# Two heads' keys summed while the tokens still land, with products of the identity ahead of them

## The chip, the cores and the metric

The kernel runs on one core of a Trainium2 chip. The metric is the device time of one execution in microseconds (us). The engines of a core work side by side, each through its own queue in order: TensorE (PE, matrix products, with its weight loads shown as PEld), VectorE (DVE), ScalarE (ACT), GpSimd (POOL), and SyncE (SP), which here only issues transfers (DMAs).

## What is computed

The kernel is one decoder block on 16 meta tokens and 512 tokens (528 in all) of width 1024. The part that matters here is its beginning: a root-mean-square norm, one large projection, and of that projection the gated-delta branch with 8 heads.

```python
n = _rmsnorm(h, pre_mix_norm[l])
proj = jnp.einsum('btd,dn->btn', n, w_in[l])
(gq, gk, gv, gz, gb, ga, aq, ak, av, iq, ik, iw, gate_a, gate_b) = jnp.split(proj, split_at, axis=-1)
...
qkv = jax.nn.silu(_causal_conv(jnp.concatenate([q, k, v], axis=-1), conv_w))
...
k = _l2norm(k)
beta = jax.nn.sigmoid(b_raw)
g = -jnp.exp(a_log) * jax.nn.softplus(a_raw + dt_bias)
...
gc = jnp.cumsum(g, axis=-1)
decay = jnp.exp(jnp.where(tri_incl, gc[..., :, None] - gc[..., None, :], -jnp.inf))
A = jnp.where(tri_strict, jnp.einsum('bhncd,bhnsd->bhncs', kb, k) * decay, 0.0)
```

Sparse attention, the merge and the MLP follow; the change doesn't touch them.

## The kernel before

Tokens lie transposed: `xr` holds 8 slices of 128 channels by 528 tokens, landing as 8 transfers of 264 KB. For each slice `k`, ACT writes its scaled high part `nhi`, DVE the remainder `nlo`, and POOL or ACT the square `sq`, which DVE sums into `sqs`. The norm's factor per token is not applied to the input; it is computed later from `sqs` and multiplied into the results as the row vector `rb`.

Weights come by `wload`: SP loads up to 512 KB into one of two buffers `raw`, ACT casts the high part (`hi_...`, line 99), DVE subtracts for the low part (`lo_...`, line 100). A projection (`proj_a`, lines 194 to 196) makes three products per slice, high by high, high by low and low by high, for each half of the tokens (264 columns): 48 products for one tile of up to 128 output columns. PE's results go to PSUM, in a ring of three buffers for projections (`pp`) and one of five for the rest (`sp`).

In order of the program: the "small columns" (`misc`, 88 columns: the index key, the raw beta and decay inputs, the index weights); from `sqs` the norm's factors (`ssn`, line 152, and the square-root chain on DVE), spread into `rb` by the products `pc` and `pb` (lines 164 to 168); from the small columns beta and the decay `gg` with a chain of small DVE operations (lines 223 to 240); its cumulated sums by the products `gcp` (lines 245 to 248). From these, POOL's queue writes `gcd` to memory and reads it back broadcast as the eight tiles `E` (line 273) and, behind them, `zsp` (line 276), from which DVE makes the decay's exponents (`decay_abs`, lines 282 and 119; `zsp`, line 277).

Meanwhile `keys(h)` projects the keys of head `h` (`pa_k`), copies them out (line 297), multiplies by `rb` (line 299), runs the convolution of four taps (ACT line 300, three DVE operations, line 303), silu and square on ACT (lines 305 and 328), and the norm's products `kss` (line 335). All silus wait until the last exponential of the decay's chain (`last_exp`) is done. The values (`pa_v`) come next.

The order of instructions on each engine is made when the kernel is built: a scheduler orders by priorities and its own estimates, and `issue_after` keeps one behind another. On the chip the order of each queue is fixed.

Of the kernel before, what the change touches and what calls it, by code (L numbers as in the profile page):

```python
# [31 lines left out]
TOPK = 128  # L32
IDX_H = 8
IDX_D = 64
S4 = {"a": 4 * T, "b": 4 * L}


@with_exitstack
def hybrid_block(ctx: ExitStack, tc: tile.TileContext, io: dict):
# [6 lines left out]
    def f(ap):  # L46
        return ap.bitcast(F32)
# [12 lines left out]
    def ptile(name, p=None):  # L60
        return (p or pp).tile([P, 512], F32, tag="ps", name=name)
# [122 lines left out]
    def proj_a(w, name, moving=None, m=P, full=True, first=0):  # L184

        hi, lo = w
        mh, ml, base = moving if moving is not None else (nhi, nlo, 0 if full else NM)
        marks.clear()
        n2 = (T - first) // 2
        parts = [(ptile(f"pa_{name}_{i}"), first + i * n2, n2) for i in range(2)] if full else [(ptile(f"pa_{name}"), 0, L)]  # L190
        for pt, c, n in parts:
            for k in range(KT):
                ws, ms = slice(k * m, (k + 1) * m), slice(base + c, base + c + n)
                TE.matmul(pt[:m, :n], hi[:, ws], mh[:, k, ms], start=(k == 0), stop=False)  # L194
                TE.matmul(pt[:m, :n], hi[:, ws], ml[:, k, ms], start=False, stop=False)  # L195
                mark = TE.matmul(pt[:m, :n], lo[:, ws], mh[:, k, ms], start=False, stop=(k == KT - 1))  # L196
                if k == KT - 1:
                    marks.append(mark)
        return parts


    misc = const("misc", [96, T])
    G.memset(misc[64:96, :], 0.0)
    for pt, c, n in proj_a(w_misc, "misc", m=88):
        S.copy(misc[:88, c : c + n], pt[:88, :n])
    scp = stile("scp")
    for t in range(1, 5):
        c, n = tokcols(t)
# [79 lines left out]
    def conv(g, c0, parts_of, out, name, wide=False):

        if wide:  # L290
            both = wk.tile([P, 2, T], F32, tag="tb", name=f"cb_{name}", bufs=2)
            cv, y = both[:, 0, :], both[:, 1, : T - c0]
        else:
            cv = wk.tile([P, T], F32, tag="cv", name=f"cv_{name}", bufs=2)
            y = wk.tile([P, T], F32, tag="y", name=f"cy_{name}", bufs=2)[:, : T - c0]
# [937 lines left out]
```

## Time and profile before

| | |
|---|---|
| three runs | 1062.56, 1062.84, 1065.58 us; median 1062.84 |
| the profiled execution | 1063.86 us, its span 1062.2 us from first to last instruction |
| PE busy | 1040.1 us, 98% of the span, 6249 products |
| DVE busy | 682.0 us, 64% |
| ACT busy | 460.9 us, 43% |
| POOL busy | 61.7 us, 6% |
| DMA | 96.44 MB |

Busy time says how long an engine had something running. Of an engine with 98% only the few stretches where it idles or runs slowly can shrink, so one looks for where these are: PE's busy share is under nine tenths only in the first and the last of 40 slices of the span.

### The profile page before, as it was taken

What the parts mean: (1) busy time and instruction counts of PE and PEld (TensorE: products, weight loads), DVE (VectorE), ACT (ScalarE), POOL (GpSimd) and SP (SyncE); (2) the same over time, 40 slices, a digit from 0 to 9 for tenths busy, and PEclk for the clock granted to TensorE, in tenths of its full rate; (3) what the DMA queues carried; (4) which work ended last, traced back from release to release, by engine and by line L of the source; (5) the groups of instructions that cost most, each with busy time, mean ns of one, the idle gap of its engine ahead of it and who ended that gap; (6) DMA issues with size and microseconds to landing.
All of it is one profiled execution on the core that took longest, in us unless ns stands there. A gap on an engine that the chain in (4) does not pass through costs nothing.

```text
span 1062.2 us, 15893 instructions
## 1 busy us (share of the span) xinstructions
PE 1040.1 (98%) x6249; PEld 900.7 (85%) x6249; DVE 682.0 (64%) x1502; ACT 460.9 (43%) x854; POOL 61.7 (6%) x85
## 2 busy tenths in 40 slices
PE   6999999999999999999999999999999999999996
PEld 6999999999997888898888888898888888888885
DVE  6797899516789999857967464794431343343346
ACT  5555565443268722346755332473432431242131
POOL 4202302100000000000000000000000000000022
PEclk9999999998999999999999999999999999999999
DMA  5433424210123133322111325133233323332332
GB/s 180 134 102 95 124 86 134 63 41 2 41 83 117 46 94 99 100 80 80 60 60 41 99 93 204 60 103 95 84 96 99 96 85 98 99 90 88 99 99 80
DMA packets 28235, 96.44 MB, mean 91 GB/s; under 512 B 3632, under 2 KB 3968, under 8 KB 28160
## 3 DMA queue, kind: packets, MB, share of 16 engines
q1 hardware_dynamic: 25440, 87.51, 26.5%
q0 software_dynamic: 2720, 7.92, 2.9%
q8 instruction: 49, 0.80, 0.3%
q14 instruction: 26, 0.21, 0.1%
HBM read 90.14 MB, written 5.28 MB: 90 GB/s over the span
## 4 chain that ended last, share of the span: by engine, by line
PE 89%; DVE 5%; ACT 2%; DMA 2%; issue 1%; SPq 0%; DVEq 0%; ACTq 0%
PE up L1103 5%; PE up L1104 5%; PE up L1102 5%; PE d L505 4%; PE d L504 4%; PE d L506 4%; PE pa_dense L891 2%; PE pa_dense L890 2%; PE pa_dense L889 2%; PE pa_q L196 1%; PE pa_q L194 1%; PE pa_q L195 1%; PE pa_bg L194 1%; PE pa_bg L196 1%; PE pa_bg L195 1%; PE bd L1012 1%
## 5 line engine op out<-in xcount | busy, mean ns | idle before, releaser
L1103 PE MATMUL up<-n2l,hi_up 128*128 128x512 f32 (+1 forms) x288 | 106.9, 372 | 0.0
L1102 PE MATMUL up<-n2h,hi_up 128*128 128x512 f32 (+1 forms) x288 | 106.6, 371 | 0.0
L1104 PE MATMUL up<-n2h,lo_up 128*128 128x512 f32 (+1 forms) x288 | 106.6, 371 | 0.0
L100 DVE TENSOR_TENSOR lo_up<-raw_up,hi_up 128x1024 fp32r<-128x1024 f32 x32 | 39.2, 1226 | 71.1 <-PE up L1103 52.9
L100 DVE TENSOR_TENSOR lo_d<-raw_d,hi_d 128x1024 fp32r<-128x1024 f32 x24 | 29.4, 1227 | 78.4 <-PE d L505 56.0
L504 PE MATMUL d<-hi_d,uh 128*128 128x512 f32 x192 | 75.9, 396 | 0.0
L506 PE MATMUL d<-hi_d,ul 128*128 128x512 f32 x192 | 75.9, 395 | 0.0
L505 PE MATMUL d<-lo_d,uh 128*128 128x512 f32 x192 | 75.9, 395 | 0.0
L1106 ACT ACTIVATE rup<-up 128x512 f32<-128x512 f32 (+1 forms) x36 | 19.9, 552 | 99.5 <-PE up L1104 99.4
L1103 PEld LDWEIGHTS up<-n2l,hi_up 128*128 128x128 f32 x288 | 54.2, 188 | 10.3
L1102 PEld LDWEIGHTS up<-n2h,hi_up 128*128 128x128 f32 x288 | 54.2, 188 | 10.3
L1104 PEld LDWEIGHTS up<-n2h,lo_up 128*128 128x128 f32 x288 | 54.1, 188 | 10.3
L99 ACT CAST hi_d<-raw_d 128x1024 fp32r<-128x1024 f32 x24 | 25.2, 1050 | 59.6 <-PE d L506 59.6
L99 ACT CAST hi_up<-raw_up 128x1024 fp32r<-128x1024 f32 x32 | 33.4, 1045 | 24.6 <-PE d L506 22.7
L504 PEld LDWEIGHTS d<-hi_d,uh 128*128 128x128 f32 x192 | 36.1, 188 | 8.8
L506 PEld LDWEIGHTS d<-hi_d,ul 128*128 128x128 f32 x192 | 36.1, 188 | 8.7
L505 PEld LDWEIGHTS d<-lo_d,uh 128*128 128x128 f32 x192 | 36.1, 188 | 8.7
L889 PE MATMUL pa_dense<-nhi,hi_dense 128*128 128x512 f32 x96 | 39.3, 409 | 0.0
L890 PE MATMUL pa_dense<-nlo,hi_dense 128*128 128x512 f32 x96 | 38.0, 396 | 0.0
L548 PE MATMUL pb_z<-hi_z,nhi 128*128 128x256 f32 x128 | 38.0, 297 | 0.0
L891 PE MATMUL pa_dense<-nhi,lo_dense 128*128 128x512 f32 x96 | 38.0, 396 | 0.0
L194 PE MATMUL pa_k<-nhi,hi_k 128*128 128x264 f32 x128 | 37.1, 290 | 0.0
(570 smaller groups left out, 3075.6 us busy)
## 6 DMA issues: line engine op xcount, KB each, us to landing
raw_up<-w_up SPq DMA_DIRECT2D x32, 512.0 KB, 3.6
raw_d<-w_down SPq DMA_DIRECT2D x24, 512.0 KB, 3.6
raw_k<-w_k SPq DMA_DIRECT2D x8, 512.0 KB, 4.6
raw_v<-w_v SPq DMA_DIRECT2D x8, 512.0 KB, 4.4
raw_q<-w_q SPq DMA_DIRECT2D x8, 512.0 KB, 3.6
raw_z<-w_z SPq DMA_DIRECT2D x8, 512.0 KB, 3.6
raw_w_ga<-w_ga SPq DMA_DIRECT2D x8, 512.0 KB, 3.6
raw_bg<-w_bg SPq DMA_DIRECT2D x8, 512.0 KB, 3.6
```

The costliest lines, as they stand in the source:

```text
L99: S.copy(hi[:, :n], raw[:, :n])
L100: V.tensor_tensor(lo[:, :n], raw[:, :n], f(hi[:, :n]), ALU.subtract)
L194: TE.matmul(pt[:m, :n], hi[:, ws], mh[:, k, ms], start=(k == 0), stop=False)
L504: TE.matmul(pt, lh, whi, start=beg, stop=False)
L505: TE.matmul(pt, lh, wlo, start=False, stop=False)
L506: TE.matmul(pt, ll, whi, start=False, stop=end)
L889: TE.matmul(pt, hi[:, ws], nhi[:, k, NM:], start=(k == 0), stop=False)
L890: TE.matmul(pt, hi[:, ws], nlo[:, k, NM:], start=False, stop=False)
L891: mm = TE.matmul(pt, lo[:, ws], nhi[:, k, NM:], start=False, stop=(k == KT - 1))
L1102: TE.matmul(pt, hi[:, ws], n2h[:, k, ms], start=(k == 0), stop=False)
L1103: TE.matmul(pt, hi[:, ws], n2l[:, k, ms], start=False, stop=False)
L1104: TE.matmul(pt, lo[:, ws], n2h[:, k, ms], start=False, stop=(k == KT - 1))
```

## The change

The keys of heads 0 and 1 (`NHEAD = 2`) are no longer projected by `keys(h)`. Their weights come with those of the small columns in four pieces (`head_weights`: 176 columns of `w_misc` and 512 of `w_k`, 352 KB in two transfers), one ahead of every second slice of tokens. As a slice lands, PE adds its part to the sums of the small columns and of both heads (`head_part`, `heads`: 6 products each), in six PSUM buffers `hd00` to `hd21`, for slices 0 to 3. For slices 4 to 7 it adds only the small columns' part; the heads' parts of those four follow behind slice 7. `issue_after(last_head.ins)` holds these products to that order, and 26 products of the identity by itself stand ahead of them. The small columns' sums and the heads' sums are then copied out, the latter to the buffers of the convolution (`conv_columns`).

```diff
+    heads = [(0, 88)] + [(2 * 88 + 2 * P * i, P) for i in range(NHEAD)]
+    hps = [[ptile(f"hd{i}{x}", sp if 2 * i + x < 3 else pp) for x in range(2)] for i in range(NHEAD + 1)]
+    for _ in range(26):
+        last_head = TE.matmul(hps[NHEAD][1][:, :P], ident, ident, start=True, stop=True)
+    def head_weights(k):
+        n = 2 * 88 + 2 * P * NHEAD
+        raw = wp.tile([P, 1024], F32, tag="raw", name=f"raw_head{k}", bufs=2)
+        nc.sync.dma_start(raw[:, : 2 * 88], io["w_misc"][:, k * 88 : (k + 2) * 88])
+        nc.sync.dma_start(raw[:, 2 * 88 : n].rearrange("p (h c) -> p h c", h=NHEAD), io["w_k"][:NHEAD, :, k * P : (k + 2) * P].rearrange("h p c -> p h c"))
+        hi, lo = HW[k // 2]
+        S.copy(hi[:, :n], raw[:, :n])
+        V.tensor_tensor(lo[:, :n], raw[:, :n], f(hi[:, :n]), ALU.subtract)
...
+    def head_part(i, k):
+        nonlocal last_head
+        o, m = heads[i]
+        hi, lo = HW[k // 2]
+        ws = slice(o + k % 2 * m, o + k % 2 * m + m)
+        for x in range(2):
+            ms = slice(x * HT, x * HT + HT)
+            for a, b in ((hi, nhi), (hi, nlo), (lo, nhi)):
+                with tc.issue_after(last_head.ins):
+                    mm = TE.matmul(hps[i][x][:m, :HT], a[:, ws], b[:, k, ms], start=(k == 0 and a is hi and b is nhi), stop=(k == KT - 1 and a is lo))
+        last_head = mm
     for k in range(KT):
         nc.sync.dma_start(xr[:, k, :], io["hT"][:, k, :])
-        if k == 0:
-            w_misc = wload(io["w_misc"], 8 * 88, "misc")
+        if k % 2 == 0:
+            head_weights(k)
...
+        for i in range(NHEAD + 1) if k < KT // 2 else (0,):
+            head_part(i, k)
...
-    for pt, c, n in proj_a(w_misc, "misc", m=88):
-        S.copy(misc[:88, c : c + n], pt[:88, :n])
+    for x in range(2):
+        S.copy(misc[:88, x * HT : x * HT + HT], hps[0][x][:88, :HT])
+    for i in range(1, NHEAD + 1):
+        for k in range(KT // 2, KT):
+            head_part(i, k)
+    headc = []
+    for i in range(NHEAD):
+        headc.append(conv_columns(f"k{i}"))
+        for x in range(2):
+            S.copy(headc[i][0][:, x * HT : x * HT + HT], hps[1 + i][x][:, :HT])
...
     def keys(h):
-        w = wload(io["w_k"][h], 1024, f"k{h}")
-        parts = proj_a(w, f"k{h}")
-        later(1, 0)
-        sq = conv(8 + h, 0, parts, kT[:, h, :], f"k{h}", wide=h % 4 > 1)
+        if h < NHEAD:
+            sq = conv(8 + h, 0, [], kT[:, h, :], f"k{h}", columns=headc[h])
+        else:
+            parts = proj_a(wload(io["w_k"][h], 1024, f"k{h}"), f"k{h}")
+            later(1, 0)
+            sq = conv(8 + h, 0, parts, kT[:, h, :], f"k{h}", wide=h % 4 > 1)
```

Three places show how the scheduler's order moves. First PE where the norm's sums `ssn` are made. Before, they stand among the products of head 0's second half:

```order
L194 MATMUL pa_k0_1_348<-nhi_98,hi_k0_343 128x264
L195 MATMUL pa_k0_1_348<-nlo_99,hi_k0_343 128x264
L152 MATMUL ssn_212<-one_84,sqs_101 16x1
L152 MATMUL ssn_212<-one_84,sqs_101 128x1 x4
L196 MATMUL pa_k0_1_348<-nhi_98,lo_k0_344 128x264
```

After, behind all products of the head (the last is that of `hd21`) and the transposes of the small columns, `scp`; the next products are those of head 2:

```order
L161 MATMUL hd21_110<-nhi_98,lo_head3_144 128x264
L260 MATMUL scp_360<-ident_78,misc_300 128x32 x4
L261 MATMUL scp_360<-ident_78,misc_300 16x32
L188 MATMUL ssn_368<-one_84,sqs_101 16x1
L188 MATMUL ssn_368<-one_84,sqs_101 128x1 x4
L230 MATMUL pa_k2_0_517<-nhi_98,hi_k2_513 128x264
```

So `ssn` and all that hangs on it stand behind two whole heads, where before they stood inside the first. `gcp` moves too, from among head 2's products to behind the third product of head 4.

Second, DVE around the low part of head 6's weights, `lo_k6`. Before, from the low part of head 5's weights to that of head 6's:

```order
L100 TENSOR_TENSOR lo_k5_705<-raw_k5_702,hi_k5_704 128x1024
L303 SCALAR_TENSOR_TENSOR cb_k3_613<-cb_k3_613,convw_92 128x527
L277 TENSOR_TENSOR zsp_326<-zsp_326,gc_292 16x128
L303 SCALAR_TENSOR_TENSOR cb_k3_613<-cb_k3_613,convw_92 128x526
L119 TENSOR_SCALAR zsp_326<-zsp_326 16x128
L303 SCALAR_TENSOR_TENSOR cb_k3_613<-cb_k3_613,convw_92 128x525
L282 TENSOR_TENSOR E_317<-E_317,gc_292 128x512
L299 TENSOR_TENSOR cv_k4_687<-cv_k4_687,rb_100 128x528
L119 TENSOR_SCALAR E_317<-E_317 128x512
L282 TENSOR_TENSOR E_317<-E_317,gc_292 128x512
L100 TENSOR_TENSOR lo_k6_784<-raw_k6_781,hi_k6_783 128x1024
```

After, the same stretch is longer: its first part runs from `lo_k5` and the first tile of `E` to the last tap of head 4, and the second from there over `zsp` to `lo_k6`:

```order
L101 TENSOR_TENSOR lo_k5_741<-raw_k5_738,hi_k5_740 128x1024
L333 TENSOR_TENSOR E_473<-E_473,gc_448 128x512
L350 SCALAR_TENSOR_TENSOR cb_k3_649<-cb_k3_649,convw_92 128x527
L346 TENSOR_TENSOR cv_k4_723<-cv_k4_723,rb_100 128x528
L350 SCALAR_TENSOR_TENSOR cb_k3_649<-cb_k3_649,convw_92 128x526
L120 TENSOR_SCALAR E_473<-E_473 128x512
L350 SCALAR_TENSOR_TENSOR cb_k3_649<-cb_k3_649,convw_92 128x525
L350 SCALAR_TENSOR_TENSOR y_k4_724<-cv_k4_723,convw_92,y_k4_724 128x527
L333 TENSOR_TENSOR E_473<-E_473,gc_448 128x512
L350 SCALAR_TENSOR_TENSOR y_k4_724<-cv_k4_723,convw_92,y_k4_724 128x526
L120 TENSOR_SCALAR E_473<-E_473 128x512
L350 SCALAR_TENSOR_TENSOR y_k4_724<-cv_k4_723,convw_92,y_k4_724 128x525
```

```order
L328 TENSOR_TENSOR zsp_482<-zsp_482,gc_448 16x128
L346 TENSOR_TENSOR cv_k5_802<-cv_k5_802,rb_100 128x528
L120 TENSOR_SCALAR zsp_482<-zsp_482 16x128
L333 TENSOR_TENSOR E_473<-E_473,gc_448 128x512 x2
L350 SCALAR_TENSOR_TENSOR y_k5_803<-cv_k5_802,convw_92,y_k5_803 128x527
L120 TENSOR_SCALAR E_473<-E_473 128x512
L350 SCALAR_TENSOR_TENSOR y_k5_803<-cv_k5_802,convw_92,y_k5_803 128x526
L120 TENSOR_SCALAR E_473<-E_473 128x512
L350 SCALAR_TENSOR_TENSOR y_k5_803<-cv_k5_802,convw_92,y_k5_803 128x525
L101 TENSOR_TENSOR lo_k6_820<-raw_k6_817,hi_k6_819 128x1024
```

Before, `lo_k6` stands ahead of head 4's taps, with three tiles of `E` begun; now it stands behind four tiles of `E`, `zsp` and all taps of heads 4 and 5.

Third, PE where head 6 begins. Before:

```order
L196 MATMUL pa_k5_1_709<-nhi_98,lo_k5_705 128x264
L335 MATMUL kss3_758<-one_84,cb_k3_613 16x1
L335 MATMUL kss3_758<-one_84,cb_k3_613 128x1 x4
L194 MATMUL pa_k6_0_787<-nhi_98,hi_k6_783 128x264
L195 MATMUL pa_k6_0_787<-nlo_99,hi_k6_783 128x264
L196 MATMUL pa_k6_0_787<-nhi_98,lo_k6_784 128x264
```

After:

```order
L232 MATMUL pa_k5_1_745<-nhi_98,lo_k5_741 128x264
L230 MATMUL pa_k6_0_823<-nhi_98,hi_k6_819 128x264
L231 MATMUL pa_k6_0_823<-nlo_99,hi_k6_819 128x264
L230 MATMUL pa_k6_1_824<-nhi_98,hi_k6_819 128x264
L384 MATMUL kss3_794<-one_84,cb_k3_649 16x1
L384 MATMUL kss3_794<-one_84,cb_k3_649 128x1 x4
L231 MATMUL pa_k6_1_824<-nlo_99,hi_k6_819 128x264
L230 MATMUL pa_k7_0_901<-nhi_98,hi_k7_897 128x264
L232 MATMUL pa_k6_0_823<-nhi_98,lo_k6_820 128x264
```

The products that need no low part, one of head 7 among them, have moved ahead of the first that reads `lo_k6`. From the values of head 0 on, the orders of PE before and after are the same but for one row.

## Rows read from the trace of the kernel before

**Rows 1.** The page's first part, PE alone: busy us, share of the span, instructions.

```profile
PE 1040.1 (98%) x6249; PEld 900.7 (85%) x6249; DVE 682.0 (64%) x1502; ACT 460.9 (43%) x854; POOL 61.7 (6%) x85
```

**Rows 2.** Busy time by stretches, here that in which the tokens land: from:to and length in us, then busy us and instructions of PE, PEld, DVE, ACT and POOL, the clock that the records give, the share of DMA time and GB/s.

```profile
6.50:13.40 6.90, 4.68 (x17) 3.58 (x18) 5.25 (x5) 4.71 (x8) 3.06 (x8) 1.00 0.96 358
```

**Rows 3.** PE in order of time: start us, duration us, line, product, form; in brackets the idle time before and what ended it. Between 30.33 and 33.11 lie 23 steps from product to product.

```profile
6.51 0.52 PE L194 MATMUL pa_misc<-nhi,hi_misc 128*88 128x264 f32 x1 [6.51 <-ACT hi_misc L99]
...
10.46 0.52 PE L195 MATMUL pa_misc<-nlo,hi_misc 128*88 128x264 f32 x1 [1.16 <-DVE nlo L136]
...
11.21 0.42 PE L196 MATMUL pa_misc<-nhi,lo_misc 128*88 128x264 f32 x1
...
12.31 0.42 PE L195 MATMUL pa_misc<-nlo,hi_misc 128*88 128x264 f32 x1
...
13.73 0.45 PE L194 MATMUL pa_misc<-nhi,hi_misc 128*88 128x264 f32 x2
...
17.92 0.24 PE L209 MATMUL scp<-ident,misc 32*128 32x32 f32 x1
...
18.86 0.39 PE L196 MATMUL pa_k<-nhi,lo_k 128*128 128x264 f32 x1
...
22.83 1.19 PE L152 MATMUL ssn<-one,sqs 128*16 128x1 f32 x10
23.87 0.37 PE L196 MATMUL pa_k<-nhi,lo_k 128*128 128x264 f32 x1
...
28.19 0.39 PE L166 MATMUL pc<-dg,tri 16*128 16x16 f32 x2
...
30.33 0.28 PE L195 MATMUL pa_k<-nlo,hi_k 128*128 128x264 f32 x1
...
33.11 0.28 PE L194 MATMUL pa_k<-nhi,hi_k 128*128 128x264 f32 x1
...
36.00 0.41 PE L245 MATMUL gcp<-gg,tri 128*128 128x32 f32 x2 [0.17 <-DVE gg L240]
...
36.94 0.39 PE L194 MATMUL pa_k<-nhi,hi_k 128*128 128x264 f32 x1
...
76.00 1.19 PE L335 MATMUL kss<-one,cy_k 128*16 128x1 f32 x10
```

**Rows 4.** DVE, ACT and POOL in order of time in the same columns, while the tokens land.

```profile
6.49 0.89 DVE L100 TENSOR_TENSOR lo_misc<-raw_misc,hi_misc 128x704 fp32r<-128x704 f32 x1
8.76 2.32 DVE L136 SCALAR_TENSOR_TENSOR nlo<-xr,gT,nhi 128x528 fp32r<-128x528 f32 x2 [1.37 <-ACT nhi L135]
...
8.77 1.07 POOL L138 TENSOR_TENSOR sq<-xr 128x528 f32<-128x528 f32 x1 [2.92 <-DMA xr<-hT]
...
10.59 0.74 ACT L135 ACTIVATE nhi<-xr,gT 128x528 fp32r<-128x528 f32 x1 [0.70 <-DMA xr<-hT]
...
14.81 0.76 DVE L136 SCALAR_TENSOR_TENSOR nlo<-xr,gT,nhi 128x528 fp32r<-128x528 f32 x1
15.49 0.70 DVE L142 TENSOR_TENSOR sqs<-sqs,sq 128x528 f32<-128x528 f32 x1
16.11 0.76 DVE L136 SCALAR_TENSOR_TENSOR nlo<-xr,gT,nhi 128x528 fp32r<-128x528 f32 x1
```

**Rows 5.** DVE in order of time in the chain from `ssn` to `gcp`.

```profile
25.82 1.22 DVE L100 TENSOR_TENSOR lo_k<-raw_k,hi_k 128x1024 fp32r<-128x1024 f32 x1
...
31.69 1.13 DVE L234 SCALAR_TENSOR_TENSOR t<-t,t 128x40 f32<-128x40 f32 x5
```

**Rows 6.** The transfers of `E` and `zsp` in POOL's queue, and DVE where it first waits for each.

```profile
42.53 6.02 POOL L273 DMA_DIRECT2D E<-gcd  x8 [2.38 <-DMA gcd<-gts]
...
47.83 0.69 DVE L282 TENSOR_TENSOR E<-E,gc 128x512 f32<-128x512 f32 x1 [2.50 <-DMA E<-gcd]
...
48.54 0.53 POOL L276 DMA_DIRECT2D zsp<-gcdm  x1
...
55.41 0.28 DVE L277 TENSOR_TENSOR zsp<-zsp,gc 16x128 f32<-16x128 f32 x1 [1.15 <-DMA zsp<-gcdm]
```

**Rows 7.** DVE in order of time, a stretch without a wait: the step from one start to the next is the price of an operation.

```profile
56.30 0.21 DVE L119 TENSOR_SCALAR zsp<-zsp 16x128 int32<-16x128 int32 x1
56.44 0.75 DVE L303 SCALAR_TENSOR_TENSOR cb_k<-cb_k,convw 128x525 f32<-128x525 f32 x1
57.11 0.67 DVE L282 TENSOR_TENSOR E<-E,gc 128x512 f32<-128x512 f32 x1
57.72 0.69 DVE L299 TENSOR_TENSOR cv_k<-cv_k,rb 128x528 f32<-128x528 f32 x1
58.33 0.41 DVE L119 TENSOR_SCALAR E<-E 128x512 int32<-128x512 int32 x1
58.67 0.67 DVE L282 TENSOR_TENSOR E<-E,gc 128x512 f32<-128x512 f32 x1
59.27 1.21 DVE L100 TENSOR_TENSOR lo_k<-raw_k,hi_k 128x1024 fp32r<-128x1024 f32 x1
```

**Rows 8.** First the stretch of the recurrence in which the records show another clock (columns as in rows 2); then the products `gp` of 128 columns in plain float32 from the chain of waits (start, us, products), and POOL's making of the identity.

```profile
240.00:248.00 8.00, 8.00 (x35) 7.43 (x36) 3.74 (x12) 2.37 (x5) 0.00 (x0) 0.50 0.00 0
...
77.18 3.68 PE gp L360 x32
...
1.23 0.29 POOL L72 TENSOR_SCALAR_AFFINE_SELECT ident<-ident 128x128 f32<-128x128 f32 x1
```

More of the change, by code (lines that the diff above doesn't have):

```diff
@@ L34 @@
 IDX_D = 64
+NHEAD = 2
 S4 = {"a": 4 * T, "b": 4 * L}
@@ L130, in hybrid_block @@
     sq = [slots.tile([P, 4096], F32, tag=("s5", "s6")[x], name=f"sq{x}")[:, : 4 * T].rearrange("p (k t) -> p k t", t=T) for x in range(2)]
+    heads = [(0, 88)] + [(2 * 88 + 2 * P * i, P) for i in range(NHEAD)]
[10 more added lines that the diff above has]
+        V.tensor_tensor(lo[:, :n], raw[:, :n], f(hi[:, :n]), ALU.subtract)
+    HW = [[wp.tile([P, 1024], F32R, tag="hl", name=f"{x}_head{k}", bufs=5) for x in ("hi", "lo")] for k in range(2)]
+    HW += [[wk.tile([P, 1024], F32R, tag="tb", name="hi_head2", bufs=2)] + [cst.tile([P, 1024], F32R, tag="st", name=f"{x}_head{k}", bufs=2) for x, k in (("lo", 2), ("hi", 3))]]
+    HW += [[HW[2].pop(), wp.tile([P, 1024], F32R, tag="hl", name="lo_head3", bufs=5)]]
+    def head_part(i, k):
[9 more added lines that the diff above has]
+        last_head = mm
     for k in range(KT):
         nc.sync.dma_start(xr[:, k, :], io["hT"][:, k, :])
-        if k == 0:
-            w_misc = wload(io["w_misc"], 8 * 88, "misc")
+        if k % 2 == 0:
+            head_weights(k)
         S.activation(nhi[:, k, :], xr[:, k, :], AF.Copy, scale=gT[:, k : k + 1])
@@ L199, in proj_a, with conv_columns @@
         return parts
+    def conv_columns(name, wide=False):
+        if wide:
+            both = wk.tile([P, 2, T], F32, tag="tb", name=f"cb_{name}", bufs=2)
+            return both[:, 0, :], both[:, 1, :]
+        return [wk.tile([P, T], F32, tag=x, name=f"{x}_{name}", bufs=2) for x in ("cv", "y")]
     misc = const("misc", [96, T])
     G.memset(misc[64:96, :], 0.0)
-    for pt, c, n in proj_a(w_misc, "misc", m=88):
-        S.copy(misc[:88, c : c + n], pt[:88, :n])
+    for x in range(2):
[8 more added lines that the diff above has]
+            S.copy(headc[i][0][:, x * HT : x * HT + HT], hps[1 + i][x][:, :HT])
     scp = stile("scp")
@@ L286, in hybrid_block, with conv @@
     silu = []
[L288 to L295, printed above, removed]
+    def conv(g, c0, parts_of, out, name, wide=False, columns=None):
+        cv, y = columns or conv_columns(name, wide)
+        y = y[:, : T - c0]
         for pt, c, n in parts_of:
             S.copy(cv[:, c : c + n], pt[:, :n])
-        f0 = parts_of[0][1]
+        f0 = c0 and c0 - 4
         V.tensor_tensor(cv[:, f0:], cv[:, f0:], rb[:, f0:], ALU.mult)
```

## The prediction

> **What bounds the kernel now.** I read the busy times first: PE runs 98% of the span [rows 1], so time can go only where PE idles or runs slowly. Then the busy time by stretches: while the tokens land PE is busy 4.68 of 6.90 us [rows 2]. PE in order of time says why. Its first product waits until 6.51, and there a product follows the last in 0.22 us (11.21 to 12.31, five steps); later in 0.121 us (23 steps from 30.33 to 33.11) [rows 3]. 264 columns in 0.22 us is TensorE's lower level, 1.2 GHz, whatever the clock column says there. So about 11 us at the start hold half a dozen us of products, and the change aims at the right place. But the tokens' own chain fills those us on DVE, ACT and the transfers, and what comes off it (the norm, the decay, the low parts of weights) is what PE needs next. Those have to be followed to the end of the keys, where before PE starts `kss` of head 5 at 76.00 [rows 3]. After it the order of PE's products is the same in both but for one row, so the difference there is the forecast.
>
> **The change, part by part.** I number from landmarks: H, the end of the head's products; X, the first product of head 2; T, the start of `gcp`. Before, T is 36.00 [rows 3].
>
> *Until H.* The products stay the same in number, 144 (48 for the small columns, 96 for two heads), so PE needs 17.4 us for them at 0.121. The identity's 26 products are new. The trace has no such product this early; the nearest are those of `gp`, 32 records of 128 columns in 3.68 us, 0.115 each, two records to a product [rows 8]. 52 records take 6.0 us, or 12.0 at half the clock, from 1.52, where the identity is made [rows 8]: they end between 7.5 and 13.5, about 9.3 if the clock rises on the way as it did before. PE alone would allow H between 24.9 and 30.9, near 26.7.
>
> DVE allows less. Per slice it makes `nlo` (0.68 from start to start) and adds to `sqs` (0.62); beside POOL's product on the same slice the two `nlo` from 8.76 took 2.32 together, some 0.85 more than two such steps [rows 4]. The low part of a weight piece was 0.89 long for 704 columns; less the 0.08 by which rows overlap, 0.81 [rows 4]. The second piece of weights lands about when the slice after it did before, 10.59 [rows 4], plus 0.2 for its size; with 0.8 for the cast its low part starts at 11.6. From there DVE's order has three low parts, five `nlo` and six sums up to the last `nlo`, without a gap: 2.43 + 3.40 + 3.72 + 0.85 = 10.4, so 22.0. Behind it PE has 54 products, 6.5 us: H = 28.5. I take this, as DVE's queue has no slack; its ends are PE's 24.9 (everything else hidden) and 30.9.
>
> The transfers are the same bytes as before up to the weights of head 1, in smaller rows; SP now waits for the first and second low parts before the third and fourth piece, and the last slices queue behind these. That puts the last slice's landing near 17, and it is needed for `nlo` at 21: hidden, by about 4 us. Casts on ACT replace casts of the same columns. Were the transfers 4 us slower still, H would begin to move.
>
> *H to X.* `scp` and `ssn` now stand bare on the path: 17.92 to 18.86 less two products is 0.7, 22.83 to 23.87 is 1.1 with its start [rows 3]. X = 30.4. Before, `ssn` was done at 23.87: all that follows from it is 6.5 us later.
>
> *X to T.* `pc` came 4.3 us after `ssn` [rows 3] with a low part of 1.1 between [rows 5], which now is done earlier: 3.2, while PE has 24 products, 2.9, so a wait of 0.3. 99 products (12.0), `pc` and `pb` (28.19 to 30.33 less five products, 1.5) and that wait bring PE to X + 13.8. The decay's chain took 7.8 us from `pc` to `gcp` [rows 3]; on DVE it now has three taps, a multiplication and a low part more in it (3 × 0.67 + 0.61 + 1.13 = 3.8) [rows 7], less 0.6, since five small operations that filled a wait (31.69) [rows 5] now lie between large ones: X + 3.2 + 11.0 = X + 14.2. So T = 44.6, a wait of 0.4 us.
>
> *T to the end of the keys.* Nothing shortens POOL's chain to `E` and `zsp`. Before, the first `E` came at T + 11.83 (47.83, where DVE waited 2.50) and `zsp` at T + 19.41 (55.41, waited 1.15) [rows 6]; eight issues in 6.02 us stand between. DVE's order now puts eleven operations from the first `E` ahead of `zsp` (two subtractions, two sign operations, six taps, a multiplication: 1.22 + 0.68 + 4.02 + 0.61 = 6.5 [rows 7]), so it arrives there at T + 18.4, and waits to T + 19.4. Behind `zsp` stand 0.2 + 0.61 + 0.14 + 2 × 0.61 + 3 × 0.67 + 2 × 0.34 = 4.9, then `lo_k6` with 1.2 [rows 7]: done at T + 25.5. PE gets there much sooner: 0.9 for `gcp` [rows 3], 96 products (45 of head 4, 48 of head 5, 3 of head 6), 11.6, 0.3 for the transpose, three `kss` of 1.1: T + 16.2; `kss` of head 3 and one product, T + 17.5. There it waits, first for `hi_k7` (ACT's cast stands behind a tap that needs what follows `zsp`), then for `lo_k6`: **8 us, with one product in it**. Before, `lo_k6` began at 59.27 [rows 7], ahead of PE's need, and nothing waited. Behind the wait 91 products (11.0) and one `kss` (1.1) bring head 5's `kss` to T + 37.6 = 82.2. Against 76.00 that is **+6.2**.
>
> *The clock.* After a pause PE's products begin at 1.2 GHz in the only long pause that the rows show, the start [rows 3]: from 10.46 they ran closely until the step fell at 13.73, so half of these 3.3 us, 1.6, is lost. The recurrence shows the other bound: 8 us at 0.50 (1.2 GHz) between narrow products [rows 8], 4.0 lost. Nothing lost is the lower bound. I take 1.6, the nearer row, as the pause here too is an idle one: +7.8.
>
> Here a rule of the Trainium skill speaks against the change: "TensorE: Matmul & The Clock Gate", section "HAM oscillation — how this bites in real kernels", says that waits for data between bursts of products put the clock back to half. By it the pause costs more than its own length; without it the sum is +6.2. The start of this trace agrees (0.22 against 0.121), and no row shows a pause later on.
>
> **Sum.** 1063.86 of the profiled execution + 7.8 = 1071.7; the median is 1.0 under that execution, so **1070.7**.
>
> **The rivals.** *A shorter head.* The identity's products warm the clock early and DVE is faster than its rows say: H = 24.9 instead of 28.5 takes 3.6 off, about +2.6 with the pause and no loss of clock, 1065.4. For it: the clock did rise early before. Against: DVE's sum has no wait in it. *Slow clock.* The identity stays at half, H = 30.9 (+2.4), or the pause costs 4.0: 1073 to 1075.4. *No pause* (the other side): `lo_k6` is done before PE needs it. Then head 5's `kss` stands at T + 29.7 = 74.3, 1.7 under before: 1061.1, and with the short head 1057.5. It decides at T + 17.5: all of `E` and `zsp` would have to come 8 us earlier relative to `gcp`. For it: DVE waited for only the first `E` and `zsp`. Against: the first `E` alone comes at T + 11.83 by a chain of two transfers, and 12 us of DVE stand between it and `lo_k6`'s end.
>
> **How the numbers follow.** A measurement of this kernel tells 0.3%, 3.2 us, from no change. Forecast, 1067 to 1074: 0.60. Shorter head, 1064.5 to 1067: 0.14. Slow clock, 1074 to 1076: 0.12. No pause: 0.10, two thirds of it within 0.3%. Something worse: 0.04. The range from 1064.5 to 1076 takes the first three, 0.86. Slower is 0.60 + 0.12 + 0.04 and 0.09 of the shorter head, 0.85; same 0.05 + 0.07 = 0.12; faster 0.03.
>
> **What would show it.** In the changed profile: the last `nlo` ending near 22 and the first product of head 2 near 30.4; `gcp` near 44.6; PE idle by about 8 us near 62 to 70 with `hi_k7` and `lo_k6` as releasers; DVE idle some 6 us before the first `E` near 56; `kss` of head 5 near 82 to 84; from there both traces alike. I am wrong if PE shows no idle time at `lo_k6`, or if `gcp` starts before 41.

## The result and the profile after

| | before | after |
|---|---|---|
| median | 1063.96 us (4 runs, 1062.56 to 1065.58) | 1073.37 us (4 runs, 1072.25 to 1074.31) |
| profiled execution, its span | 1063.86, 1062.2 us | 1074.31, 1072.6 us |

The ratio is 1.0087, with a 95% interval from 1.0066 to 1.0109: slower by 9.4 us between the medians, 10.4 between the profiled executions. The prediction was 1070.7, with a range from 1064.5 to 1076: the direction is right, the size 2.7 too small.

First the busy times, against [rows 1].

```profile
PE 1050.7 (98%) x6301; PEld 912.3 (85%) x6301; DVE 684.4 (64%) x1503; ACT 460.4 (43%) x855; POOL 62.9 (6%) x85
```

PE has 52 records more, the identity's, and is busy 10.6 us longer: 8.5 of that are these products. Where the rest went, PE in order of time says (start, duration, and in brackets the idle time ahead), against [rows 3].

```profile
1.57 8.54 PE L137 MATMUL hd<-ident 128*128 128x128 f32 x52 [1.57 <-POOL ident L73]
...
21.60 0.35 PE L161 MATMUL hd<-nhi,lo_head 128*88 128x264 f32 x1 [1.03 <-DVE lo_head L146]
22.90 0.35 PE L161 MATMUL hd<-nlo,hi_head 128*88 128x264 f32 x1 [0.46 <-DVE nlo L169]
...
29.32 0.28 PE L161 MATMUL hd<-nhi,lo_head 128*128 128x264 f32 x1
...
30.97 0.37 PE L230 MATMUL pa_k<-nhi,hi_k 128*128 128x264 f32 x1
...
45.64 0.31 PE L296 MATMUL gcp<-gg,tri 128*128 128x32 f32 x2
...
52.06 1.19 PE L384 MATMUL kss<-one,y_k 128*16 128x1 f32 x10
...
53.65 1.30 PE L384 MATMUL kss<-one,y_k 128*16 128x1 f32 x10
...
57.29 2.01 PE L384 MATMUL kss<-one,cb_k 128*16 128x1 f32 x10
...
71.23 0.39 PE L230 MATMUL pa_k<-nhi,hi_k 128*128 128x264 f32 x1 [2.84 <-ACT hi_k L100]
74.25 0.59 PE L232 MATMUL pa_k<-nhi,lo_k 128*128 128x264 f32 x1 [2.64 <-DVE lo_k L101]
...
88.59 1.19 PE L384 MATMUL kss<-one,y_k 128*16 128x1 f32 x10
```

`gcp` starts at 45.64 instead of 36.00, 9.6 late, and `kss` of head 5 at 88.59 instead of 76.00, 12.6 late. The pause for `hi_k7` and `lo_k6` stands at the forecast place in PE's order, 2.84 and 2.64 us long, though some 6 us later than forecast. The third part of the loss has no bracket. A `kss` is five products with a moving operand of one column, two records each; at 57.29 these ten records take 2.01, where a `kss` took 1.18 or 1.19 before. The first two groups also stood further apart before, 5.0 us where it is 1.6 now. PE in order of time, of the kernel before:

```profile
42.89 1.19 PE L335 MATMUL kss<-one,cy_k 128*16 128x1 f32 x10
...
47.86 1.19 PE L335 MATMUL kss<-one,cy_k 128*16 128x1 f32 x10
```

The busy times by stretches of the changed kernel name the loss (from:to and length, busy us of PE, PEld, DVE, ACT and POOL, then the granted clock):

```profile
54.00:56.00 2.00, 2.00 (x13) 2.00 (x13) 0.00 (x0) 1.04 (x5) 2.00 (x4) 0.64 0.71 115
56.00:64.00 8.00, 8.00 (x39) 7.75 (x38) 3.88 (x7) 3.21 (x9) 1.75 (x3) 0.50 0.78 225
64.00:66.00 2.00, 2.00 (x15) 2.00 (x15) 2.00 (x4) 1.03 (x2) 0.00 (x0) 0.80 0.00 0
70.00:72.00 2.00, 0.39 (x1) 0.19 (x1) 1.73 (x4) 1.17 (x2) 0.00 (x0) 0.91 0.00 0
72.00:78.00 6.00, 3.75 (x17) 3.75 (x18) 6.00 (x11) 1.29 (x2) 0.00 (x0) 0.50 0.29 89
78.00:80.00 2.00, 2.00 (x16) 2.00 (x16) 1.90 (x9) 0.83 (x1) 0.00 (x0) 0.89 0.79 223
252.00:254.00 2.00, 2.00 (x11) 1.71 (x11) 1.72 (x6) 1.75 (x4) 0.00 (x0) 0.64 0.00 0
254.00:258.00 4.00, 4.00 (x19) 3.77 (x19) 1.11 (x5) 0.58 (x1) 0.00 (x0) 0.50 0.00 0
258.00:260.00 2.00, 2.00 (x14) 2.00 (x14) 1.42 (x6) 0.00 (x0) 0.00 (x0) 0.66 0.00 0
```

From about 54.6 to 64.8 PE is busy without a gap, at 0.50 of its clock (1.2 GHz). A stretch of 2 us at 0.64 holds 1.44 us of it and one at 0.80 holds 0.80, so these are 10.2 us, and 5.1 of them lost. After the pause some 4.2 us of products run at 0.50, 2.1 lost. The last three rows are the recurrence's own slow stretch: 6.8 us here against 10.2 before ([rows 8] show its core), which gives 1.7 back; two waits before `vtp`, the transposes of the values behind the keys, are shorter by 0.4. So 12.6 late at `kss` of head 5 became 10.4 at the end.

DVE in order of time, against [rows 4], [rows 6] and [rows 7]:

```profile
22.09 0.76 DVE L169 SCALAR_TENSOR_TENSOR nlo<-xr,gT,nhi 128x528 fp32r<-128x528 f32 x1
...
56.97 0.69 DVE L333 TENSOR_TENSOR E<-E,gc 128x512 f32<-128x512 f32 x1 [6.46 <-DMA E<-gcd]
...
60.12 0.71 DVE L346 TENSOR_TENSOR cv_k<-cv_k,rb 128x528 f32<-128x528 f32 x1 [1.78 <-ACT cv_k L344]
...
63.89 0.77 DVE L350 SCALAR_TENSOR_TENSOR y_k<-cv_k,convw,y_k 128x527 f32<-128x527 f32 x1 [1.37 <-ACT y_k L347]
...
66.87 0.27 DVE L328 TENSOR_TENSOR zsp<-zsp,gc 16x128 f32<-16x128 f32 x1
...
72.98 1.22 DVE L101 TENSOR_TENSOR lo_k<-raw_k,hi_k 128x1024 fp32r<-128x1024 f32 x1
```

`E` and `zsp` stand ahead of `lo_k6` as forecast. But DVE waits 1.78 and 1.37 us for ACT, which stands waiting for PE's products at half clock (2.98 us for `kss` of head 2, 1.81 for columns of `pa_k`), and reaches `zsp` at 66.87, when its transfer (issued at 57.23, 6.7 us to landing) has been there for some 3 us.

### The profile page after: what moved, and what is told of

Its sections match the earlier page's. It is cut to its first block, busy times and chain, and to the rows that moved or that the text cites. A ratio compares the mean times of both kernels' runs of the same rounds, so it can differ in the third digit from the quotient of the medians.

```text
span 1072.6 us, 16008 instructions
## 1 busy us (share of the span) xinstructions
PE 1050.7 (98%) x6301; PEld 912.3 (85%) x6301; DVE 684.4 (64%) x1503; ACT 460.4 (43%) x855; POOL 62.9 (6%) x85
## 4 chain that ended last, share of the span: by engine, by line
PE 86%; DVE 7%; ACT 3%; DMA 2%; issue 1%; SPq 0%; DVEq 0%; ACTq 0%
PE up L1153 5%; PE up L1152 5%; PE up L1151 5%; PE d L555 4%; PE d L553 4%; PE d L554 4%; PE pa_dense L939 2%; PE pa_dense L940 2%; PE pa_dense L938 2%; PE pb_z L597 1%; PE pa_q L230 1%; PE pa_q L232 1%; PE pa_q L231 1%; PE pa_bg L230 1%; PE bd L1060 1%; PE bd L1059 1%
## 5 line engine op out<-in xcount | busy, mean ns | idle before, releaser
L1152 PEld LDWEIGHTS up<-n2l,hi_up 128*128 128x128 f32 x288 | 54.2, 188 | 10.3
L1151 PEld LDWEIGHTS up<-n2h,hi_up 128*128 128x128 f32 x288 | 54.2, 188 | 10.3
L1153 PEld LDWEIGHTS up<-n2h,lo_up 128*128 128x128 f32 x288 | 54.1, 188 | 10.3
L100 ACT CAST hi_up<-raw_up 128x1024 fp32r<-128x1024 f32 x32 | 33.4, 1045 | 24.9 <-PE d L555 22.7
L230 PE MATMUL pa_v<-nhi,hi_v 128*128 128x264 f32 x128 | 37.1, 289 | 0.0
```

The costliest lines, as they stand in the source:

```text
L1151: TE.matmul(pt, hi[:, ws], n2h[:, k, ms], start=(k == 0), stop=False)
L1152: TE.matmul(pt, hi[:, ws], n2l[:, k, ms], start=False, stop=False)
L1153: TE.matmul(pt, lo[:, ws], n2h[:, k, ms], start=False, stop=(k == KT - 1))
```

## The experiments

My theory was **the late norm**: `ssn` waits for the whole head, `gcp` comes 9.6 late, and pause and slow stretches follow from that. Against it stood that DVE has too much of the head's own work, and, for the busy stretch at 0.50, that it has a cause of its own. All ratios are to the kernel before, on the same chip.

**norm_first: the norm ahead of the heads' last products.**

```diff
     for x in range(2):
         S.copy(misc[:88, x * HT : x * HT + HT], hps[0][x][:88, :HT])
-    for i in range(1, NHEAD + 1):
-        for k in range(KT // 2, KT):
-            head_part(i, k)
...
     scp = stile("scp")
...
     rn, scale_rows = token_scales()
...
     scale_rows()
+    for i in range(1, NHEAD + 1):
+        for k in range(KT // 2, KT):
+            head_part(i, k)
...
```

The copies `headc` move with the loop.

> The changed kernel with the two heads' products of the last four slices, and the copies of their columns, moved in the program behind the transposes `scp`, the norm `ssn` and the rows `pc`, `pb`; all else as it was. Theory (the late norm): `gcp` stood 9.6 us later than before (45.64 against 36.00) only because `ssn` waited for all of the head's products, and the pause at `hi_k7` and `lo_k6` (5.5 us) and the two stretches at half clock (some 7 us of lost products) follow from that. Then here `ssn` comes near 24.5 instead of 29.9, `gcp` near 38, no pause, kss of head 5 near 74.5 (29.4 for the head, 3.3 for scp, ssn, pc and pb, 284 products of 0.121, 5 kss of 1.1, 1.2 for gcp and gtp) instead of 88.6, and the time is near 1061 (1059 to 1064), no slower than before. Rival (too much on DVE): the low parts and taps of the head itself put lo_k6 behind; then the pause stays at 4 us or more and the time is above 1067.

Measured: 1068.81, ratio 1.0053 (1.0040 to 1.0066). The pause and the slow stretch at the keys are gone, as the theory says, though `gcp` came only at 41.55. The time is missed (it lies where the rival put it, without the rival's pause), by a new wait. PE in order of time:

```profile
26.09 0.31 PE L252 MATMUL scp<-ident,misc 32*128 32x32 f32 x1 [2.82 <-ACT misc L248]
...
41.55 0.38 PE L296 MATMUL gcp<-gg,tri 128*128 128x32 f32 x2 [0.38 <-DVE gg L291]
...
80.93 1.19 PE L384 MATMUL kss<-one,y_k 128*16 128x1 f32 x10
```

ACT in order of time, where `misc` is copied:

```profile
24.71 1.04 ACT L100 CAST hi_k<-raw_k 128x1024 fp32r<-128x1024 f32 x1 [3.15 <-DMA raw_k<-w_k]
25.67 0.65 ACT L248 COPY misc<-hd 88x264 f32<-88x264 f32 x2
```

The busy times of the stretch behind the wait, with the granted clock behind POOL's count:

```profile
26.00:32.00 6.00, 5.91 (x28) 5.49 (x29) 3.98 (x20) 0.31 (x2) 0.00 (x0) 0.50 0.38 128
```

The copy of `misc` stood on ACT behind a cast that waited 3.15 us for weights; in the changed kernel this was covered by the head's 48 products. The wait of 2.82 cost 3 us more in clock: 5.9 us of products at 0.50.

**one_identity: 1 product of the identity instead of 26.**

```diff
-    for _ in range(26):
+    for _ in range(1):
```

> The changed kernel with 1 product of the identity in place of 26. Theory (DVE bounds the head): PE waited 1.03 us for a low part at 21.60 and 0.46 for the last nlo at 22.90, so products at half clock between about 9.5 and 13 are made good before that; the head ends near 29.4 to 30.4 as with them, and the time stays within 1.5 us of 1073.4. Rival (the identity is worth its place): without it the clock stays at half through the head's first pieces, the head ends 3 us or more later, and the time is 1076 or more.

Measured: 1072.11, ratio 1.0089 (1.0073 to 1.0104), the same as with them. PE in order of time:

```profile
7.99 0.52 PE L161 MATMUL hd<-nhi,hi_head 128*88 128x264 f32 x1 [5.62 <-ACT hi_head L145]
...
29.40 0.43 PE L260 MATMUL scp<-ident,misc 32*128 32x32 f32 x4
```

The head starts at 7.99 at half clock (a product follows the last in 0.22 us up to 14.06) and still ends as in the changed kernel (`scp` at 29.40 against 29.53): the identity's products buy nothing here.

**kss_apart: the narrow products of heads 1 to 3 put off.**

```diff
...
-            parts = proj_a(wload(io["w_k"][h], 1024, f"k{h}"), f"k{h}")
-            later(1, 0)
+            parts = proj_a(wload(io["w_k"][h], 1024, f"k{h}"), f"k{h}", between=h in (5, 6))
+            later({3: 2, 4: 3, 5: 2}.get(h, 1), 0)
```

With `between`, one `kss` is issued between the two halves of a head.

> The changed kernel with the narrow products `kss` of heads 1 to 3 put off, so that 24 or more products stand between one head's kss and the next, instead of 3 between those of heads 0 and 1 and 9 before that of head 2. Theory (narrow products in a row): the granted clock of 0.50 from 54.8 to 65 in a stretch where PE never idles comes of those narrow products; here it stays at 1.00 there. PE then reaches lo_k6 some 5 us sooner and waits longer, DVE's waits for the copies (1.78 and 1.37 us) go, lo_k6 is done some 3 us sooner, kss of head 5 comes near 85.5 instead of 88.6 and the time is near 1070.5. Rival (the clock falls for another reason, such as the wait at 45.42): it is at 0.50 for some 10 us in that place here too, and the time stays at 1073 to 1074.

Measured: 1073.70 (1071.97 to 1080.02), ratio 1.0108 (1.0082 to 1.0135). The clock, and `kss` of head 5, are as the theory says: 1.00 from 56 to 65, and 85.74. PE in order of time:

```profile
66.17 0.59 PE L230 MATMUL pa_k<-nhi,hi_k 128*128 128x264 f32 x1 [3.67 <-ACT hi_k L100]
69.64 0.59 PE L232 MATMUL pa_k<-nhi,lo_k 128*128 128x264 f32 x1 [2.88 <-DVE lo_k L101]
...
85.74 1.19 PE L386 MATMUL kss<-one,y_k 128*16 128x1 f32 x10
```

The busy times of that stretch:

```profile
56.00:65.00 9.00, 6.50 (x54) 5.95 (x52) 7.46 (x14) 5.45 (x13) 1.26 (x3) 1.00 0.62 180
```

The time is not: of the 2.9 us won at the keys more than half was given back behind them (the span is 1.2 shorter, with a new wait of 1.4 for `hi_iq`), and four runs that spread over 8 us do not resolve the rest. So the time neither bears the theory out nor speaks against it.

**decay_behind: the work on E behind the keys.**

```diff
     for h in range(NH):
         keys(h)
-        if h > 3:
-            decay_abs(2 * h - 8)
-            decay_abs(2 * h - 7)
+    for h in range(NH):
+        decay_abs(h)
     products(0)
```

> The changed kernel with all subtractions and sign operations on E put into the program behind the keys of all heads; by DVE's order lo_k6 and lo_k7 then stand ahead of the operation on zsp. Theory: the pause at hi_k7 and lo_k6 (5.5 us) is DVE's queue behind E and zsp and nothing else; here it is gone, with the half clock that followed it (some 2 us), kss of head 5 comes near 81 to 82 instead of 88.6, gcp stays near 45.6, the slow stretch at 55 to 65 stays, and the time is near 1066 to 1067. Rival (given back): the work on E, now later, holds up the operations on lhs and what needs them, so that waits of PE before the transposes vtp grow by as much as was gained, and the time stays at 1071 or more.

Measured: 1066.18, ratio 1.0044 (1.0024 to 1.0063). The pause is gone and the time as expected, but not by the expected sum. PE in order of time:

```profile
76.04 1.19 PE L384 MATMUL kss<-one,y_k 128*16 128x1 f32 x10
...
83.11 0.39 PE L232 MATMUL pa_v<-nhi,lo_v 128*128 128x264 f32 x1 [1.72 <-DVE lo_v L101]
...
91.34 0.39 PE L230 MATMUL pa_v<-nhi,hi_v 128*128 128x264 f32 x1 [1.51 <-ACT hi_v L100]
```

The busy times of the stretch that was slow in the changed kernel:

```profile
56.00:65.00 9.00, 9.00 (x76) 8.81 (x76) 7.77 (x12) 5.78 (x15) 1.49 (x3) 1.00 0.84 245
```

`kss` of head 5 stands at 76.04, where it stood before the change, because here the stretch from 55 to 65 ran at 1.00, with the `kss` of heads 0, 1 and 2 as close together as in the changed kernel. That the time came out as expected is luck: 5 us more were won at the keys than expected, and some 3.4 given back behind them, where the work on `E`, now later, makes `lo_v` and `hi_v` late. Of its six executions four took 1065.7 to 1066.2 with a mean clock of 0.995, two took 1070.6 and 1072.6 with 0.989 and 0.987. These two were not profiled. The fall of the clock at the keys is thus not in every execution of one order: it is in the profile of the changed kernel and not in this one.

**narrow_doubled and narrow_apart: is it the narrow products?** Both change decay_behind, one by computing the `kss` of heads 0 to 2 twice, the other by the edit of kss_apart. They ran on another chip than decay_behind.

```diff
...
-        for t in range(5):
+        for t in (0, 1, 2, 3, 4, 0, 1, 2, 3, 4) if h < 3 else range(5):
```

> decay_behind with each `kss` of heads 0, 1 and 2 computed twice in place (5 narrow products more for each, some 1.1 us each, 3.3 in all); the profile of decay_behind had the clock at 1.00 there, and so, by their mean clock of 0.995, had four of its six runs, while two had 0.987 and 0.989 and were 4.4 to 6.4 us longer. Theory (narrow products close together make the clock fall): with twice as many it falls in all or nearly all runs, the mean clock is 0.990 or less, and the time is 1074 to 1075 (1066.2 + 3.3 + some 5). Rival (they do not): the clock is 0.994 or more in most runs, as in decay_behind, and the time is 1069 to 1070.

> decay_behind with the kss of heads 1 to 3 put off as in kss_apart, so that 24 or more products stand between one head's kss and the next. Theory (narrow products close together make the clock fall): no run has the fall at the keys; the mean clock is 0.994 or more in all of them, the time is 1065.5 to 1066.5, none above 1068. Rival (the fall comes by chance or of something else): about one run in three has a clock of 0.987 to 0.989 and is 4 to 6 us longer, as in decay_behind.

Measured: doubled 1076.05, ratio 1.0115 (1.0102 to 1.0129), and all four executions have a mean clock of 0.988 or 0.989. Apart 1065.27, ratio 1.0013 (1.0003 to 1.0024), and of twelve executions none is above 1066.74. The same stretch with the narrow products doubled:

```profile
56.00:65.00 9.00, 9.00 (x45) 8.72 (x46) 2.78 (x5) 3.07 (x9) 1.03 (x2) 0.52 0.55 162
```

And with them apart:

```profile
56.00:65.00 9.00, 9.00 (x76) 8.53 (x75) 7.28 (x11) 4.54 (x11) 1.38 (x3) 1.00 0.94 264
```

With twice the narrow products the mean clock was low in all four executions, and the one profiled has the fall. Apart, one part of the expectation failed: seven of the twelve have a mean clock of 0.990 to 0.993, not 0.994, and took 1065.1 to 1066.7 where four of the other five took 1061.9 to 1063.7. Only one of the seven was profiled (0.993), and it has 1.00 throughout the keys. Five have 0.992 or less; as the profiles with 0.991 and 0.990 (decay_chain_first, norm_first) hold 14 and 17 us at 0.50 and this one 11, I estimate that those five hold up to 6 us more of it, and where is not known. So the twelve times alone do not show that the fall is gone.

The profiles of all the kernels together say more. In seven of them the first two groups of `kss` start close together, 1.6 to 2.0 us apart (2.7 in narrow_doubled, where a group takes twice as long); in five of these the clock fell behind them while PE was busy (the changed kernel, one_identity, sums_behind, decay_chain_first, narrow_doubled), in two not (decay_behind, norm_hidden). In the six where they start 4.5 us or more apart (before, one_head, norm_first, kss_apart, narrow_apart, all_moves) it never fell at the keys while PE was busy. That narrow products close together make the fall more likely is borne out; that they suffice is not, and what decides in the single execution stays open.

**norm_hidden: the norm early, and nothing in its way.** As norm_first, with two more slices of the head ahead of `scp`, the cast of head 3 behind the copies of `misc`, and its low part behind `sc`.

```diff
+    rest = [(i, k) for i in range(1, NHEAD + 1) for k in range(KT // 2, KT)]
+    for i, k in rest[:2]:
+        head_part(i, k)
     scp = stile("scp")
...
     scale_rows()
+    for i, k in rest[2:]:
+        head_part(i, k)
...
+        with tc.issue_after(after[0].ins) if after else ExitStack():
             S.copy(hi[:, :n], raw[:, :n])
+        with tc.issue_after(after[1].ins) if after else ExitStack():
             V.tensor_tensor(lo[:, :n], raw[:, :n], f(hi[:, :n]), ALU.subtract)
```

> As norm_first, but without the wait of 2.82 us that stood there before `scp` (the copy of `misc` on ACT lay behind a cast that waited for weights): the copies of misc go ahead of the cast of head 3, `scp` and `ssn` stand behind two more slices (12 products) of the head, the low part of head 3 behind the multiplications of `sc`. Theory (the late norm): no wait of PE at scp and no stretch at half clock near 25 to 33; `ssn` near 25, `pc` near 29, `gcp` near 39.5 to 40.5 (by PE's order it stands 65 products behind pc); no pause at the keys, kss of head 5 near 74.5 against 76.00 before, and the time is 1060 to 1063. Rival: DVE or ACT are late with something else of the head, a new wait of 2 us or more stands ahead of gcp, and the time is above 1065.

Measured: 1063.40, ratio 0.9999 (0.9991 to 1.0008): the whole loss is gone, which is the theory's main claim, though the time is 0.4 above the expected 1060 to 1063. `gcp` and `kss` of head 5 came 1 to 2 and 3 us later than expected, with waits of PE for DVE ahead of them:

```profile
41.38 0.38 PE L301 MATMUL gcp<-gg,tri 128*128 128x32 f32 x2 [0.60 <-DVE gg L296]
...
57.91 0.39 PE L234 MATMUL pa_k<-nhi,lo_k 128*128 128x264 f32 x1 [1.04 <-DVE lo_k L103]
...
77.52 1.19 PE L389 MATMUL kss<-one,y_k 128*16 128x1 f32 x10
```

**decay_chain_first: priority for the decay's operations.** As norm_hidden, with

```diff
+    with tc.high_priority(offset=600):
+        S.activation(t1, sc[:, :, 0:8], AF.Tanh, scale=0.5)
...
+        G.dma_start(gcdm, gts[:NH, P : P + NM])
```

> As norm_hidden, with the operations from `beta` to the transfers of `gts` given priority over the heads' taps: by the order, gcp stands 14 rows sooner on PE than there. Theory (what matters is only whether E is there before DVE's queue needs it): gcp comes 1.5 to 2 us sooner than in norm_hidden, and since no product waits for E in either, the times agree within 1 us. Rival: E is still what the keys wait for; then this one is faster by the 1.5 to 2 us.

Measured: 1067.04, ratio 1.0026 (1.0017 to 1.0035): slower than norm_hidden by 3.6, which neither side of the expectation had, though `gcp` came 1.9 sooner (39.45). In the profiles `kss` of head 5 stands at 80.50 against 77.52, 3.0 later, and again it is the clock: two falls with 6.8 us at 0.50 between them, 3.4 lost. The busy times of two stretches:

```profile
50.00:56.00 6.00, 6.00 (x42) 6.00 (x41) 5.41 (x9) 2.90 (x5) 0.65 (x2) 0.79 0.83 251
56.00:65.00 9.00, 7.83 (x52) 7.45 (x50) 8.09 (x15) 4.37 (x10) 0.00 (x0) 0.81 0.17 59
```

The first fall follows `kss` of heads 0 and 1 at 45.82 and 47.77. In norm_hidden these stand even closer, at 47.58 and 49.28, and nothing fell:

```profile
50.00:56.00 6.00, 6.00 (x52) 5.84 (x51) 3.31 (x7) 3.90 (x8) 2.46 (x4) 1.00 0.90 266
```

Why the one and not the other stays open.

**one_head: one head instead of two.**

```diff
-NHEAD = 2
+NHEAD = 1
```

> The changed kernel with the keys of one head instead of two beside the small columns (the constant of their number at 1). Theory (the late norm): 24 products less and 0.26 us less for each of three low parts stand ahead of `ssn`, so it comes near 26 to 26.5 instead of 29.9 and gcp near 40 to 41 instead of 45.6; in norm_first the pause was gone with gcp at 41.55, so it is gone here, there is no stretch at half clock near 55 to 65, kss of head 5 comes near 76 to 77, and the time is 1061 to 1064.5, the same as before within 0.3%. Rival (the loss is of the way in which a head is summed, not of the late norm): half of the loss stays, 1067 to 1069.

Measured: 1064.31, ratio 1.0008 (0.9998 to 1.0019), as the theory says, with `gcp` even sooner. One of ten executions took 1068.82, with a mean clock of 0.990 where the others have 0.993 to 0.995. PE in order of time:

```profile
38.73 0.41 PE L296 MATMUL gcp<-gg,tri 128*128 128x32 f32 x2
...
77.06 1.19 PE L384 MATMUL kss<-one,y_k 128*16 128x1 f32 x10
```

**sums_behind: the sums of squares behind the low parts.**

```diff
...
-        if k:
-            V.tensor_tensor(sqs, sqs if k > 1 else sq[0][:, 0, :], sq[k // 4][:, k % 4, :], ALU.add)
+    for k in range(1, KT):
+        with tc.issue_after(nlo_last.ins):
+            V.tensor_tensor(sqs, sqs if k > 1 else sq[0][:, 0, :], sq[k // 4][:, k % 4, :], ALU.add)
```

> The changed kernel with the seven sums into `sqs` put behind the last `nlo` on DVE; the head's low parts and nlo no longer queue behind them. Theory (DVE sets the head's end): the last nlo starts near 19.2 instead of 22.09, bound by the slice's own arrival, and the head's end by PE itself (10.1 for the identity and 17.4 for 144 products): H near 27.5 instead of 29.44, `ssn` near 28, `gcp` near 43.7, and the time falls by 1.5 to 2 us, to 1071.5 to 1072. Rival (the transfers or ACT set it): the last nlo does not move by more than 1 us, H stays at 29, and the time at 1073 to 1074.

Measured: 1071.19, ratio 1.0066 (1.0048 to 1.0084); no wait of PE is left in the head, which ends 1.6 us sooner, and `gcp` moves with it. PE in order of time:

```profile
27.95 0.43 PE L262 MATMUL scp<-ident,misc 32*128 32x32 f32 x4
...
44.07 0.30 PE L298 MATMUL gcp<-gg,tri 128*128 128x32 f32 x2
```

DVE's queue set the head's end. The pause is there as before (2.85 and 2.44 us). The time is not resolved: four runs spread from 1067.30 to 1073.07 and overlap those of the changed kernel.

**all_moves: the three put together,** as its expectation lists them, with no edit of its own but `rest[:3]` for `rest[:2]`.

> decay_chain_first with the sums into sqs behind the last nlo (as in sums_behind), one more slice of the head ahead of `scp`, and the kss of heads 1 to 3 put off (as in kss_apart). Theory: each waits for something the other moves no longer hold up: no wait of PE over 0.6 us between 12 and 60, `gcp` near 38, no stretch at half clock in the keys, kss of head 5 near 75 against 76.00 before, and the time is 1060.5 to 1062.5, under that of before by 0.1 to 0.3%. Rival (DVE's queue is full from 10 to 48 us whatever the order): new waits of PE, 2 us or more in all, stand before E or the low parts, and the time is 1063.5 or more.

Measured: 1063.68, ratio 0.9999 (0.9991 to 1.0008): the same as before the change, not faster. `kss` of head 5 is 0.3 ahead of before; a wait for a low part eats what was won. PE in order of time:

```profile
53.40 0.39 PE L236 MATMUL pa_k<-nhi,lo_k 128*128 128x264 f32 x1 [1.32 <-DVE lo_k L103]
...
75.73 1.19 PE L394 MATMUL kss<-one,y_k 128*16 128x1 f32 x10
```

The two expectations share this result: no slow stretch and the early `gcp` (38.79), as the first says, and a full queue of DVE, as the rival says, though its wait is 1.3 us and not 2. No version that I ran beats the kernel before.

## Why the prediction was right in direction and too small

*Until H.* Right in kind: DVE bounds the head (sums_behind), and the identity is worth nothing (one_identity). Its products ended at 10.1, within 7.5 to 13.5. The last `nlo` ended at 22.77 instead of 22.0, H came at 29.44 instead of 28.5: 0.9 too small. DVE's own sum was right (10.3 us from the second low part on, forecast 10.4); that low part started at 12.49 instead of 11.6.

*H to X* took 1.5 instead of 1.9, *X to T* 14.7 instead of 14.2, with a wait of 0.45 for the forecast 0.4. So T was 45.64 against 44.6. That T is late against the kernel before is the cause of the loss: with the norm ahead of the head's tail (norm_hidden), or with half the tail (one_head), the loss is gone.

*T to the end of the keys.* The first `E` came at T + 11.3 (forecast 11.8). The pause was forecast from T + 17.5 to T + 25.5; it stood from T + 22.7 to T + 28.6. Both ends moved by the same unforeseen thing: PE, at half clock from 54.6 to 64.8, came 5.1 us later, and DVE, waiting for PE's columns, finished `lo_k6` 3.0 later. In kss_apart, without the slow stretch, PE resumed with `lo_k6` at T + 24.1: beside that run the slow stretch cost 4.5 here, and my sum for DVE up to there was 1.4 too long. decay_behind shows that DVE's order made the pause: without `E` and `zsp` ahead of `lo_k6` it is gone.

*The clock.* **This is the step that failed.** I let the clock fall only after an idle pause and took 1.6 for it. After the pause it cost 2.1, close. The trace agrees here with the rule of the Trainium skill that I cited ("TensorE: Matmul & The Clock Gate", section "HAM oscillation — how this bites in real kernels"), that waits between bursts of products put the clock back to half: the products behind the pause ran at 0.50. In norm_first, too, a wait of 2.82 us was followed by 6 us at 0.50. But the larger fall came while PE was busy throughout. I had such a fall in the rows ([rows 8]: 0.50 with PE busy 8.00 of 8.00, between products of 16 to 128 columns, not of one) and used it only as a bound for the pause. Of its 5.1 us some 3.0 reached the end of `lo_k6`, counted from the forecast (4.5 counted from kss_apart); the rest shortened the pause.

*After the keys* I let both traces run alike. In fact 2.2 came back, 1.7 of them from the recurrence's clock, whose slow stretch is 3.4, 6.8 or 10.2 us long in these profiles, though no experiment touches the recurrence. This was luck for the forecast: without it the changed kernel would have taken some 2 us more, above the 1067 to 1074 to which I gave most weight.

*The sum* at `kss` of head 5, against the forecast +6.2 + 1.6 = 7.8: +1.0 for T, +3.0 for `lo_k6`, +0.5 for the clock behind the pause (2.1 for 1.6), and 0.3 left over make 12.6. Less 2.2 that is 10.4.

*The rivals.* The shorter head and no pause did not happen. How the latter was priced is seen in decay_behind, where `lo_k6` is done in time and T (45.56) is that of the changed kernel: `kss` of head 5 stood at T + 30.5, forecast T + 29.7, but the time was 1066.2, not 1061.1, since T was late and 3.4 us of waits came behind the keys. norm_hidden and one_head, without the pause and with an earlier T, took 1063.4 and 1064.3; there other waits are left. Slow clock, 1073 to 1075.4, fits the time, but not the place that I gave it: it is neither the identity nor the pause alone.

## What to carry to other kernels

Work pulled forward into an idle start pushes back whatever waited for that start: here 48 products ahead of a norm cost more than the idle time they filled. With the norm ahead of most of them they cost nothing, once nothing else stood in its way (norm_hidden, not yet norm_first). Follow the chain behind the moved work on each in-order engine up to the point where the old order is restored, and ask what stood between its narrow products: when several groups of them end up side by side, price that stretch at both levels of the clock, as in most of the profiles, not all, it fell there.

## What the runs showed of the chip that I had not expected

- The granted clock fell to 0.50 (1.2 GHz) for 10.2 us while PE's records show no gap, after two groups of ten one-column records 1.6 us apart. With the groups doubled four executions of four had a low mean clock (0.988 or 0.989). Over all kernels it fell like this in five of seven profiles with the first two groups 2.7 us or less apart, and in none of six with 4.5 us or more.
- Executions of one kernel differ in it: the kernel with the pause removed took 1066 us in four executions and 1070.6 and 1072.6 in two, with mean clocks of 0.995 against 0.989 and 0.987. Where in the two the clock was low was not profiled.
- A wait of 2.82 us in the middle of the head (norm_first) was followed by 6 us at 0.50; waits of 1.03 at 21.60 (the changed kernel), 1.32 at 53.40 (all_moves) and 1.04 at 57.91 (norm_hidden) were followed by none, one of 1.17 at 59.34 in decay_chain_first was, by 3.4 us. The last two both stand 3 us behind a group of narrow products, so that does not tell them apart.
